# The first projection's contraction in two halves with partial sums in SBUF, and 32 instead of 16 modulation loads beside the next layer's grouped products

## The chip, the cores and the metric

The kernel runs on one core of one Trainium2 chip. The time is the device time of one execution in microseconds (us). TensorE is PE in the profile, VectorE DVE, ScalarE ACT, GpSimd POOL; SyncE (SP) only issues transfers.

## The reference

The reference computes a two-layer encoder trunk on x of 256 x 2048 (256 positions, width 2048) with a conditioning vector c of 2048. What matters here:

```python
cond = jax.nn.silu(c)
for layer in range(2):
    mod = cond @ ada_w[layer] + ada_b[layer]            # 2048 x 12288
    sh1, sc1, g1, sh2, sc2, g2 = jnp.split(mod, 6)
    h = rms_norm(x, norm_g[layer, 0]) * (1 + sc1) + sh1
    y = local_dilated_mixer(h, ...) if layer == 0 else diff_attention(h, ...)
    x = x + g1 * rms_norm(y, norm_g[layer, 1])
    h = rms_norm(x, norm_g[layer, 2]) * (1 + sc2) + sh2
    y = conv_ffn(h, ...)        # (gelu(conv(h @ gate)) * (h @ up)) @ w_down, inner width 5504
    x = x + g2 * rms_norm(y, norm_g[layer, 3])
# local_dilated_mixer: proj = h @ w_in (2048 x 3584), split into
#   qa 512, ka 256, va 256 (4 heads with a sink), qb 3 x 512, kb 512, vb 512
#   (4 heads, each over three dilations, merged); then o @ w_out (1024 x 2048)
```

Everything is in float32. Each of the weights is read once, about 580 MB in all.

## The kernel before

**Loads.** A `Plan` object fixes one sequence of 1104 loads of 512 KB each, and SP issues them in that order into a ring of nine buffers called `raw`. 720 of them are weight *units* (128 x 1024 numbers: four k-tiles by 256 columns, or two k-tiles by 512). A k-tile is 128 rows of the contraction, so the width 2048 has 16. The other 384 are rows of the modulation matrix `ada_w`, called a0, a1, ... below; the units are w0, w1, .... `put(nw, na, p)` appends nw units and na modulation loads, mixed with a slope p. A transfer starts when the load nine places earlier has been worked off and its buffer is free. The order of the sequence is also the order in which ACT and DVE work off the loads.

**A weight unit** is split into a high and a low part: ACT writes `whi` (L259), DVE writes `wlo` = `raw` - `whi` (L309), with four buffers of each. PE then makes three products, high by high, high by low and low by high, which is 24 matmuls of 256 columns (L655, L657, L658, `feat_units`: outputs with features on the partitions) or 12 of 512 (L622, L623, L624, `tok_units`: outputs with positions on the partitions).

**A modulation load** is multiplied by one column of silu(c) and added to an accumulator `aacc` (128 x 1024, two buffers) by one DVE instruction (L284; the first of a chunk is L280, or L305 on top of a tile made by POOL in L299). Sixteen such loads make one *chunk*. Then PE sums over the partitions (L459; L451 for gates), DVE adds bias and norm weights (L471, L474), and the `mod` columns of that chunk are there. ACT or DVE then makes `hf` = z * A + B (`Affine`, L509 on ACT, L511 on DVE), ACT `hT` high (L514), DVE `hT` low (L518), and only then can PE multiply by these k-tiles. A chunk of layer 0's first modulation (shift and scale, a0 to a63) serves four k-tiles. a64 to a95 are the gate, a96 to a159 the shift and scale ahead of the ConvFFN, again four k-tiles a chunk.

**Layer 0's first projection** has 56 units. Before, `GK` = (0, 4, 8, 12, 16): four groups of four k-tiles. In each group the six products va, v1 (two units), kb, qb0 and qb1 are advanced by one unit each, 6 units in all, and stay in six banks of PSUM. Each group waits until the loads up to `plan.mark[q]` are worked off and its chunk of modulation is done. After the fourth group the eight remaining outputs (4 units each) run over the whole contraction, with the attention heads between them, and ACT copies each finished output to SBUF (`feat_out`, L669). The output projection (16 units) ends the mixer, at unit w71.

**The ConvFFN of layer 0** starts with `PRE` = 7 products, grouped in the same manner: `FK` = (0, 8, 12, 16), 14, 7 and 7 units, w72 to w99. Of the 64 modulation loads that they need, 14 are gated into the norm between the two (`TAIL0`; eight loads, a132 to a139, are multiplied on PE by L272 rather than on DVE) and `PA` = 16 come among the products, by `PP` = [(12, 8), (7, 8)].

**Order.** Outside the blocks with a manual schedule a scheduler sets, at build time, the fixed order in which each engine takes its instructions, by rules of its own. So an instruction that waits holds up all that stands behind it on its engine.

At the start the norm weights `norm_g` for the gate are spread over 128 partitions by four matmuls (L1171) with four ACT copies into the tile `gb` (L1172).

Of the kernel before, what the change touches and what calls it, by code (L numbers as in the profile page):

```python
# [17 lines left out]
KT = D // P  # L18
# [8 lines left out]
OUT0 = [4, 5, 6, 7, 0, 1, 2, 3]  # L27
# [12 lines left out]
class Plan:  # L40


    def __init__(self, ab_w_in, ab_w_out, c_w_in, c_w_out, ffn_w_up, ffn_w_down):
        self.units = []
        self.held, self.native = set(), set()
# [10 lines left out]
        self.native = set(i for i in range(self.n_attn0 - 16) if NATIVE(i))  # L56
# [58 lines left out]
    def order(self):  # L115
# [4 lines left out]
        ns = [b - a for a, b in zip(GK, GK[1:])]  # L120
# [68 lines left out]
def encoder_kernel(ctx: ExitStack, tc: tile.TileContext, x, c, ada_w, ada_b, norm_g,  # L189
# [21 lines left out]
    class Stream:  # L211
        def __init__(self):
            self.loaded = self.used = self.cur = 0
            self.outstanding = self.direct = self.gate = 0
# [29 lines left out]
        def split(self, s, i):  # L244
            ap, a, n = units[i]
            v = self.raw.pop(s)
            if i in plan.native:
                self.direct += 1
                self.hl[i] = (v.rearrange("p (a n) -> p a n", a=a), None)
                return  # L250
# [61 lines left out]
        def advance(self, limit=None, lows=True, n=None):  # L312
# [43 lines left out]
        def free(self, i):  # L356
            if i in plan.native:
                self.direct -= 1
            elif i not in plan.held:
                self.outstanding -= 1  # L360
# [60 lines left out]
    grow = tmp.tile([P, 512], F32, name="junk", bufs=1)  # L421
    nc.sync.dma_start(grow[:4], norm_g[0, 1, :].rearrange("(k n) -> k n", k=4))
# [203 lines left out]
    def tok_units(dsts, act, ks, first=True, last=True, one_bank=False):  # L626

        n = 0
        while n < len(ks):
            i, (hi, lo) = st.take()  # L630
            a = hi.shape[1]
            for b in range(a):
                for t in range(2):
                    mm_tok(dsts[t], act, ks[n + b], t, hi[:, b], lo and lo[:, b],
# [4 lines left out]
    def feat_units(acc, k0, kn, n):  # L639
# [3 lines left out]
        while kt < k0 + kn:  # L643
            i, (hi, lo) = st.take()
            a = hi.shape[1]
            for b in range(a):
                k = kt + b
                for j in range(n // P):
                    wh = hi[:, b, j * P:(j + 1) * P]
                    if lo is None:  # L650
                        nc.tensor.matmul(acc[:, j], wh, cur["h"][:, k], start=k == 0 and j == 0, stop=k == KT - 1,
                                         skip_group_check=True)
                        continue
                    wl = lo[:, b, j * P:(j + 1) * P]
                    nc.tensor.matmul(acc[:, j], wh, hT[:, k, 0], start=k == 0 and j == 0, stop=False,  # L655
                                     skip_group_check=True)
                    nc.tensor.matmul(acc[:, j], wh, hT[:, k, 1], start=False, stop=False, skip_group_check=True)  # L657
                    nc.tensor.matmul(acc[:, j], wl, hT[:, k, 0], start=False, stop=k == KT - 1,  # L658
# [356 lines left out]
    def out_proj(oT, ks, l, head=None):  # L1015
# [12 lines left out]
        out_chunks(oT, ks, evac, *((2, 3) if l == 0 else (1, 2)),  # L1028
# [117 lines left out]
    with tc.tile_pool(name="at0", bufs=1, reuse_waits="tile") as pool:  # L1146
# [19 lines left out]
        sel = tmp.tile([P, 4, P], F32, name="hf", bufs=3)  # L1166
        nc.vector.tensor_copy(sel[:4], ident[:4, :4].unsqueeze(2).to_broadcast([4, 4, P]))
        mods[0, 2] = cp.tile([P, D], F32, name="gb")
        for k in range(4):
            b = bank()  # L1170
            nc.tensor.matmul(b, sel[:4, k], grow[:4], start=True, stop=True)  # L1171
            nc.scalar.activation(mods[0, 2][:, k * 512:(k + 1) * 512], b, AF.Copy)  # L1172
# [14 lines left out]
        va, kb0, qb0, qb1 = [packed() for _ in range(4)]  # L1187
        v1 = [bank(), bank()]
        for q, (k0, k1) in enumerate(zip(GK, GK[1:])):
            st.advance(plan.mark[q])  # L1190
            st.flush()
            n = k1 - k0
            for k in range(k0, k1, 4):
                for t in range(2):
                    Affine(t, k, zT[:, k:k + 4, t * P:(t + 1) * P], mods[0, 1], mods[0, 0], AFF0[t],
                           keep=bool(plan.native)).high().low()
            hT = cur["hT"]
            ks = list(range(k0, k1))
            end = k1 == KT
# [120 lines left out]
```

## Time and profile before

| what | value |
|---|---|
| median of three runs | 2292.65 us (2286.78, 2292.65, 2294.36) |
| the profiled execution | 2296.29 us, its span 2294.5 us |
| mean granted clock of PE | 0.985 |
| PE busy | 2214.2 us, 97% of the span |
| DVE busy | 1626.6 us, 71% |
| ACT busy | 1059.6 us, 46% |
| read from HBM | 582.58 MB, 255 GB/s over the span |

How to read it: PE is busy nearly all of the time, so a change can only win where PE idles or runs at a lower clock, and the slices of the span show that both happen at the front. Shares over the whole span say little about that front; it is read from windows.

### The profile page before, as it was taken

Reading aid. Unit: us, or ns where it says so; the run is one execution under the profiler, and the core shown is the slowest. Engines: PE = TensorE matmul, PEld = TensorE weight load, DVE = VectorE, ACT = ScalarE, POOL = GpSimd, SP = SyncE. Lnnn points to the kernel's source line nnn. Section 1 sums busy time; section 2 is a strip of 40 time slices with the busy share of each in tenths; the row PEclk is TensorE's granted clock in tenths of the full one; section 3 lists DMA queues with packets and bytes.
Section 4 is the critical chain, followed back from the end, with each engine's and each line's share of the span. In section 5 each row is a group of like instructions: output and inputs, shape, how many; then the busy total and the mean of one; then the engine's idle time right before and its main releaser. Section 6 shows DMA issues by size and latency. Waiting matters only on the chain.

```text
span 2294.5 us, 37387 instructions
## 1 busy us (share of the span) xinstructions
PE 2214.2 (97%) x14961; PEld 2030.4 (88%) x14961; DVE 1626.6 (71%) x1802; ACT 1059.6 (46%) x1451; POOL 45.3 (2%) x72
## 2 busy tenths in 40 slices
PE   5689999999999999999999999999999999999998
PEld 3679987999988999988789999779999888999986
DVE  7888987887766777876778986656656545565554
ACT  4344456544434444444644555455444444444443
POOL 0000000000000000000000110000000000000000
PEclk9889999999999999999999999999999999999999
DMA  9999998988889888987599986656666666666552
GB/s 342 359 326 325 327 315 284 313 295 286 286 291 303 287 287 289 297 290 235 173 347 324 302 300 201 219 169 184 203 195 204 197 205 209 193 203 203 177 188 102
DMA packets 390427, 587.14 MB, mean 256 GB/s; under 512 B 18110, under 2 KB 256360, under 8 KB 389612
## 3 DMA queue, kind: packets, MB, share of 16 engines
q1 hardware_dynamic: 390252, 584.75, 77.4%
q8 instruction: 117, 1.92, 0.3%
q14 instruction: 58, 0.48, 0.1%
HBM read 582.58 MB, written 2.10 MB: 255 GB/s over the span
## 4 chain that ended last, share of the span: by engine, by line
PE 80%; issue 12%; DVE 4%; DMA 3%; ACT 1%; POOL 1%; DVEq 0%; POOLq 0%; ACTq 0%
PE bank L655 16%; PE bank L657 16%; PE bank L658 16%; PE bank L622 9%; PE bank L624 9%; PE bank L623 9%; DVE aacc L284 2%; DMA raw<-in_ada_w_dram 2%; PE bank L459 1%; DVE wlo L309 1%; DMA raw<-in_ab_w_in_dram 1%; PE bank L523 1%; PE bank L831 1%; PE bank L794 0%; ACT junk L491 0%
## 5 line engine op out<-in xcount | busy, mean ns | idle before, releaser
L309 DVE TENSOR_TENSOR wlo<-raw,whi 128x1024 fp32r<-128x1024 f32 x708 | 861.2, 1219 | 488.6 <-ACT whi L259 472.6
L259 ACT ACTIVATE whi<-raw 128x1024 fp32r<-128x1024 f32 x708 | 745.6, 1055 | 998.7 <-PE bank L657 488.3
L655 PE MATMUL bank<-hT,whi 128*128 128x256 f32 x3616 | 1027.6, 284 | 0.0
L658 PE MATMUL bank<-hT,wlo 128*128 128x256 f32 x3616 | 1018.8, 282 | 5.4 <-DVE wlo L309 5.4
L657 PE MATMUL bank<-hT,whi 128*128 128x256 f32 x3616 | 1018.4, 282 | 0.1
L658 PEld LDWEIGHTS bank<-hT,wlo 128*128 128x128 f32 x3616 | 685.2, 189 | 7.1 <-DVE wlo L309 7.0
L655 PEld LDWEIGHTS bank<-hT,whi 128*128 128x128 f32 x3616 | 685.6, 190 | 3.1 <-ACT whi L259 1.2
L657 PEld LDWEIGHTS bank<-hT,whi 128*128 128x128 f32 x3616 | 685.4, 190 | 3.2 <-issue 1.7
L284 DVE SCALAR_TENSOR_TENSOR aacc<-raw,ccol,aacc 128x1024 f32<-128x1024 f32 x352 | 453.8, 1289 | 49.3 <-DMA raw<-in_ada_w_dram 47.5
L622 PE MATMUL bank<-whi,act 128*128 128x512 f32 x656 | 259.2, 395 | 0.0
L624 PE MATMUL bank<-whi,act 128*128 128x512 f32 x656 | 258.9, 395 | 0.0
L623 PE MATMUL bank<-wlo,act 128*128 128x512 f32 x656 | 258.9, 395 | 0.0
L624 PEld LDWEIGHTS bank<-whi,act 128*128 128x128 f32 x656 | 123.5, 188 | 29.2
L622 PEld LDWEIGHTS bank<-whi,act 128*128 128x128 f32 x656 | 123.5, 188 | 28.8
L623 PEld LDWEIGHTS bank<-wlo,act 128*128 128x128 f32 x656 | 123.5, 188 | 28.5
L622 PE MATMUL bank<-whi,hT 128*128 128x512 f32 (+1 forms) x192 | 76.1, 401 | 14.6 <-ACT hT L514 14.6
L623 PE MATMUL bank<-wlo,hT 128*128 128x512 f32 (+1 forms) x192 | 75.2, 394 | 0.0
L624 PE MATMUL bank<-whi,hT 128*128 128x512 f32 (+1 forms) x192 | 73.3, 391 | 0.0
L622 PE MATMUL bank<-whi,oT 128*128 128x512 f32 x176 | 71.1, 404 | 0.0
L623 PE MATMUL bank<-wlo,oT 128*128 128x512 f32 x176 | 69.6, 395 | 0.0
L624 PE MATMUL bank<-whi,oT 128*128 128x512 f32 x176 | 69.4, 395 | 0.0
L486 POOL TENSOR_TENSOR rs_r<-rs_m,mhalf 128x1 f32<-128x1 f32 x32 | 25.6, 809 | 1902.6 <-DVE rs_m L484 1902.6
(168 smaller groups left out, 1383.4 us busy)
## 6 DMA issues: line engine op xcount, KB each, us to landing
raw<-in_ada_w_dram SPq DMA_DIRECT2D x384, 512.0 KB, 5.6
raw<-in_ffn_w_up_dram SPq DMA_DIRECT2D x344, 512.0 KB, 4.7
raw<-in_ffn_w_down_dram SPq DMA_DIRECT2D x168, 512.0 KB, 4.9
raw<-in_c_w_in_dram SPq DMA_DIRECT2D x96, 512.0 KB, 5.3
raw<-in_ab_w_in_dram SPq DMA_DIRECT2D x56, 512.0 KB, 6.1
raw<-in_c_w_out_dram SPq DMA_DIRECT2D x32, 512.0 KB, 4.7
raw<-in_ab_w_out_dram SPq DMA_DIRECT2D x16, 512.0 KB, 5.8
gb<-in_norm_g_dram SPq DMA_DIRECT2D x3, 1024.0 KB, 4.8
```

Source lines behind the costliest of these rows:

```text
L259: nc.scalar.activation(hi, v, AF.Copy)
L284: nc.vector.scalar_tensor_tensor(self.acc, t, col, self.acc, op0=ALU.mult, op1=ALU.add)
L309: nc.vector.tensor_tensor(lo, v, hi.bitcast(F32), op=ALU.subtract)
L459: nc.tensor.matmul(t[:, j:j + 1], acc[:, j * P:(j + 1) * P], ones[:, 0:1], start=True, stop=rows is None)
L486: nc.gpsimd.tensor_tensor(r, m, mhalf, op=ALU.pow)
L523: nc.tensor.transpose(ps[:, q * P:(q + 1) * P], src[:, q * P:(q + 1) * P], ident)
L622: nc.tensor.matmul(dst, ah, hi, start=first, stop=False, skip_group_check=True)
L623: nc.tensor.matmul(dst, ah, lo, start=False, stop=False, skip_group_check=True)
L624: nc.tensor.matmul(dst, al, hi, start=False, stop=last, skip_group_check=True)
L655: nc.tensor.matmul(acc[:, j], wh, hT[:, k, 0], start=k == 0 and j == 0, stop=False, skip_group_check=True)
L657: nc.tensor.matmul(acc[:, j], wh, hT[:, k, 1], start=False, stop=False, skip_group_check=True)
L658: nc.tensor.matmul(acc[:, j], wl, hT[:, k, 0], start=False, stop=k == KT - 1, skip_group_check=True)
```

## The change

The projection is cut into k-tiles 0 to 7 and 8 to 15. In each half two groups of four k-tiles run, now with 7 units each (qb2 joins, so seven banks are held). After the first half ACT copies the seven partial sums to SBUF (`first_half`); then the seven outputs that before ran later run over k-tiles 0 to 7 (14 units), each copied to SBUF by ACT. In the second half each finished sum in PSUM is added to its partial sum by one DVE instruction (`second_half`), 14 in all, in place of the ACT copies. The partial sums of kb and qb0 to qb2 of the first head pair lie in the buffer `gb`; so the norm weights of the gate are loaded there later, by one transfer of 1 MB in `ada_finish`, and the matmuls and copies at the start go. Those of v lie in `vy`, where z was.

The b heads of the second pair move behind the a heads, and the output projection's k-tiles are reordered to match (`OUT0`, `late`). Code that had no effect (`NATIVE`, `DIRECT`, `keep`) goes.

Ahead of the ConvFFN, `PA` = 32 modulation loads are left for its products, which run in four groups of 7 units (`FK`); the eight loads multiplied on PE are now a116 to a123, and one of two `Affine` calls per group moves from DVE to ACT (`AFF1`).

```diff
-OUT0 = [4, 5, 6, 7, 0, 1, 2, 3]
+OUT0 = [4, 5, 0, 1, 2, 3, 6, 7]
...
-        for k0, k1 in zip(GK, GK[1:]):
-            self.rows(w_in0, k0, k1 - k0, 768, 256)
-            self.rows(w_in0, k0, k1 - k0, 3072, 512)
-            for c0 in (2560, 1024, 1536):
-                self.rows(w_in0, k0, k1 - k0, c0, 256)
-        for c0 in (2048, 2816, 1280, 1792, 2304, 512, 0, 256):
-            self.rows(w_in0, 0, KT, c0, 256)
-        self.token_chunks(w_out0, OUT0, late=2, lc=3)
+        for half in range(2):
+            for k0 in (8 * half, 8 * half + 4):
+                self.rows(w_in0, k0, 4, 768, 256)
+                self.rows(w_in0, k0, 4, 3072, 512)
+                for c0 in (2560, 1024, 1536, 2048):
+                    self.rows(w_in0, k0, 4, c0, 256)
+            for c0 in (512, 0, 256, 2816, 1280, 1792, 2304):
+                self.rows(w_in0, 8 * half, 8, c0, 256)
+        self.token_chunks(w_out0, OUT0, late=1, lc=3)
...
-        self.put(0, 4 * ns[0] - 3)
-        for q, n in enumerate(ns):
+        self.put(0, 13)
+        for nw in (5, 19, 5, 5):
             self.put(2, 0)
             self.put(0, 3)
             self.mark.append(len(self.seq))
-            if q < len(ns) - 1:
-                self.put(3 * n // 2 - 2, 4 * ns[q + 1] - 3, *TUNE1)
-        self.put(3 * ns[-1] // 2 - 2, 4)
+            if len(self.mark) < 4:
+                self.put(nw, 13, *TUNE1)
+        self.put(5, 4)
...
-PE_B, PE_N = 20, 8
-PP = [(12, 8), (7, 8)]
-PA = 16
+PE_B, PE_N = 36, 8
+PP = [(5, 0), (7, 16), (7, 16)]
+PA = 32
-FK = (0, 8, 12, 16)
-GK = (0, 4, 8, 12, 16)
-AFF0, AFF1 = (1, 1), (0, 1)
+FK = (0, 4, 8, 12, 16)
+AFF0, AFF1 = (1, 1), (1, 1)
...
-    grow = tmp.tile([P, 512], F32, name="junk", bufs=1)
-    nc.sync.dma_start(grow[:4], norm_g[0, 1, :].rearrange("(k n) -> k n", k=4))
...
-            if ms[0] == 5 and l == 1 and c0 == 0:
+            if (l, ms[0]) in ((0, 2), (1, 5)) and c0 == 0:
                 gate_rows(l, ms[0])
...
+    def first_half(dst, acc, scale=1.0):
+        nc.scalar.activation(dst, acc, AF.Copy, scale=scale)
+
+    def second_half(dst, part, acc, scale=1.0):
+        nc.vector.scalar_tensor_tensor(dst, acc, scale, part, op0=ALU.mult, op1=ALU.add)
...
+        early_groups(0)
+        for d, scale in late:
+            acc = packed()
+            feat_units(acc, 0, 8, 256, 0, 8)
+            first_half(d, acc, scale)
+        early_groups(1)
+
+        def rest(n):
+            d, scale = late[n]
+            acc = packed()
+            feat_units(acc, 8, 8, 256, 8, KT)
+            second_half(d, d, acc, scale)
...
+        pair(0, [kq0[:, g] for g in range(4)])
+        rest(0)
+        for j, qa in enumerate((qa0, qa1)):
+            rest(1 + j)
             for i in range(2):
                 attn_a(pool, i, 2 * j + i, qa[:, i], ka[:, j], v, j * P, oT, dists[0], sinkb)
+        for g in range(4):
+            rest(3 + g)
+        pair(1, kq1)
         out_proj(oT, OUT0, 0)
```

`early_groups(half)` is the loop over the two groups of a half: it waits for `plan.mark`, makes the `Affine` of both position halves, advances the seven products, and at the end calls `first_half` or `second_half` on the seven banks. The numbers of units before the four marks are 0, 6, 12 and 18 in the order of work before; they become 0, 7, 28 and 35.

The fixed order of instructions moves at three places. In these rows the line of the code stands first (the lines of the changed kernel differ by 10 to 20: L248 is `whi`, L273 and L269 `aacc`, L298 `wlo`, L453 and L456 the `mod` columns, L473 the squares of x for the norm, L491 `Affine`, L500 `hT` low, L511 normalised rows, L656 `second_half`), and x4 means four in a row.

ACT at the very start, before:

```order
L435 ACT_TABLE_LOAD
L435 ACTIVATE crow<-crow 16x128
L430 ACTIVATE dd<-dd 128x512
L1172 ACTIVATE gb<-bank 128x512 x4
L491 ACTIVATE junk,ssq<-xs 128x512 x6
L529 ACTIVATE hf<-xs,rs_r 128x512
```

and in the changed kernel:

```order
L417 ACT_TABLE_LOAD
L417 ACTIVATE crow<-crow 16x128
L473 ACTIVATE junk,ssq<-xs 128x512 x4
L412 ACTIVATE dd<-dd 128x512
L473 ACTIVATE junk,ssq<-xs 128x512 x4
L511 ACTIVATE hf<-xs,rs_r 128x512 x3
```

The four copies to `gb`, which stood ahead of the squares of x, are gone.

DVE around the chunk of modulation for the third group, before:

```order
L309 TENSOR_TENSOR wlo<-raw,whi 128x1024 x3
L284 SCALAR_TENSOR_TENSOR aacc<-raw,ccol,aacc 128x1024 x3
L471 TENSOR_TENSOR mod_338<-bank,abc 128x4
L280 TENSOR_SCALAR aacc<-raw,ccol 128x1024
L471 TENSOR_TENSOR mod_340<-bank,abc 128x4
L474 SCALAR_TENSOR_TENSOR mod_340<-mod_340,ngc 128x4
L284 SCALAR_TENSOR_TENSOR aacc<-raw,ccol,aacc 128x1024 x2
L518 TENSOR_TENSOR hT<-hf,hT 128x4x128
```

and now:

```order
L298 TENSOR_TENSOR wlo<-raw,whi 128x1024
L273 SCALAR_TENSOR_TENSOR aacc<-raw,ccol,aacc 128x1024
L453 TENSOR_TENSOR mod_330<-bank,abc 128x4
L273 SCALAR_TENSOR_TENSOR aacc<-raw,ccol,aacc 128x1024
L453 TENSOR_TENSOR mod_332<-bank,abc 128x4
L273 SCALAR_TENSOR_TENSOR aacc<-raw,ccol,aacc 128x1024
L456 SCALAR_TENSOR_TENSOR mod_332<-mod_332,ngc 128x4
L273 SCALAR_TENSOR_TENSOR aacc<-raw,ccol,aacc 128x1024 x2
L500 TENSOR_TENSOR hT<-hf,hT 128x4x128
```

Two accumulations of the next chunk, each with two inputs from SBUF, now stand between the three small instructions that finish the columns; before it was one with a single such input.

DVE in the products ahead of the ConvFFN, up to the last chunk's columns, before:

```order
L309 TENSOR_TENSOR wlo<-raw,whi 128x1024
L284 SCALAR_TENSOR_TENSOR aacc<-raw,ccol,aacc 128x1024 x2
L309 TENSOR_TENSOR wlo<-raw,whi 128x1024
L284 SCALAR_TENSOR_TENSOR aacc<-raw,ccol,aacc 128x1024
L309 TENSOR_TENSOR wlo<-raw,whi 128x1024
L284 SCALAR_TENSOR_TENSOR aacc<-raw,ccol,aacc 128x1024
L309 TENSOR_TENSOR wlo<-raw,whi 128x1024
L284 SCALAR_TENSOR_TENSOR aacc<-raw,ccol,aacc 128x1024
L471 TENSOR_TENSOR mod_2643<-bank,abc 128x4
L471 TENSOR_TENSOR mod_2645<-bank,abc 128x4
L474 SCALAR_TENSOR_TENSOR mod_2645<-mod_2645,ngc 128x4
L309 TENSOR_TENSOR wlo<-raw,whi 128x1024
```

and now:

```order
L298 TENSOR_TENSOR wlo<-raw,whi 128x1024
L273 SCALAR_TENSOR_TENSOR aacc<-raw,ccol,aacc 128x1024 x2
L298 TENSOR_TENSOR wlo<-raw,whi 128x1024
L273 SCALAR_TENSOR_TENSOR aacc<-raw,ccol,aacc 128x1024 x3
L298 TENSOR_TENSOR wlo<-raw,whi 128x1024
L273 SCALAR_TENSOR_TENSOR aacc<-raw,ccol,aacc 128x1024 x2
L453 TENSOR_TENSOR mod_2964<-bank,abc 128x4
L453 TENSOR_TENSOR mod_2966<-bank,abc 128x4
L456 SCALAR_TENSOR_TENSOR mod_2966<-mod_2966,ngc 128x4
L298 TENSOR_TENSOR wlo<-raw,whi 128x1024 x3
```

Where one accumulation stood beside each `wlo`, two or three stand now. From the 250th load on, the two load sequences are the same.

More of the change, by code (lines that the diff above doesn't have):

```diff
@@ L213, in __init__ @@
             self.loaded = self.used = self.cur = 0
-            self.outstanding = self.direct = self.gate = 0
+            self.outstanding = self.gate = 0
             self.ring_order = deque()
@@ L356, in free @@
         def free(self, i):
-            if i in plan.native:
-                self.direct -= 1
-            elif i not in plan.held:
+            if i not in plan.held:
                 self.outstanding -= 1
@@ L637, in tok_units, with feat_units @@
             st.done(i)
-    def feat_units(acc, k0, kn, n):
+    def feat_units(acc, k0, kn, n, begin=0, end=KT):
         hT = cur["hT"]
@@ L649, in feat_units @@
                     wh = hi[:, b, j * P:(j + 1) * P]
[L650 to L653, printed above, removed]
                     wl = lo[:, b, j * P:(j + 1) * P]
-                    nc.tensor.matmul(acc[:, j], wh, hT[:, k, 0], start=k == 0 and j == 0, stop=False,
+                    nc.tensor.matmul(acc[:, j], wh, hT[:, k, 0], start=k == begin and j == 0, stop=False,
                                      skip_group_check=True)
                     nc.tensor.matmul(acc[:, j], wh, hT[:, k, 1], start=False, stop=False, skip_group_check=True)
-                    nc.tensor.matmul(acc[:, j], wl, hT[:, k, 0], start=False, stop=k == KT - 1,
+                    nc.tensor.matmul(acc[:, j], wl, hT[:, k, 0], start=False, stop=k == end - 1,
                                      skip_group_check=True)
@@ L1165, in encoder_kernel @@
             to_columns(*row)
[L1166 to L1172, printed above, removed]
         new_hT()
@@ L1186, in encoder_kernel @@
                 chunk_T(t, ch, rs[t], zT[:, ch * 4:ch * 4 + 4, t * P:(t + 1) * P])
[L1187 to L1193, printed above, removed]
-                for t in range(2):
[L1195 to L1199, printed above, removed]
-            tok_units([va[:, 0], va[:, 1]], hT, ks, q == 0, end, one_bank=True)
-            tok_units(v1, hT, ks, q == 0, end)
-            if end:
-                v = pool.tile([P, 2, 768], F32, name="v") if plan.native else vy()
-                oT = pool.tile([P, 8, 2, S], F32R, name="oT")
-                nc.scalar.activation(v[:, :, 0:256], va, AF.Copy)
-                for t in range(2):
-                    nc.scalar.activation(v[:, t, 256:768], v1[t], AF.Copy)
-            feat_units(kb0, k0, n, 256)
-            if end:
-                kb = feat_out(pool, kb0, 1.0, "kb")
-                qb = []
-            for g, b in enumerate((qb0, qb1)):
-                feat_units(b, k0, n, 256)
-                if end:
-                    qb.append(feat_out(pool, b, QK_SCALE, f"qb{g}"))
@@ new lines, in encoder_kernel @@
+        hT = cur["hT"]
+        v = cur["h"].rearrange("p k n -> p (k n)")[:, :2 * 768].rearrange("p (t n) -> p t n", t=2)
+        kq0 = cp.tile([P, D], F32, name="gb").rearrange("p (g j n) -> p g j n", g=4, j=2)
+        kq1 = [pool.tile([P, 2, S], F32, name=n) for n in ("kb", "qb0", "qb1", "qb2")]
+        ka, qa0, qa1 = [pool.tile([P, 2, S], F32, name=n) for n in ("ka", "qa0", "qa1")]
+        late = [(ka, 1.0), (qa0, QK_SCALE), (qa1, QK_SCALE)]
+        late += [(d, QK_SCALE if g else 1.0) for g, d in enumerate(kq1)]
@@ new lines, in early_groups @@
+        def early_groups(half):
+            b0, e0 = 8 * half, 8 * half + 8
+            va, v1, kq = packed(), [bank(), bank()], [packed() for _ in range(4)]
+            for k0 in (b0, b0 + 4):
+                st.advance(plan.mark[k0 // 4])
+                st.flush()
+                for t in range(2):
+                    Affine(t, k0, zT[:, k0:k0 + 4, t * P:(t + 1) * P], mods[0, 1], mods[0, 0], AFF0[t]).high().low()
+                ks = list(range(k0, k0 + 4))
+                tok_units([va[:, 0], va[:, 1]], hT, ks, k0 == b0, k0 + 4 == e0, one_bank=True)
+                tok_units(v1, hT, ks, k0 == b0, k0 + 4 == e0)
+                for acc in kq:
+                    feat_units(acc, k0, 4, 256, b0, e0)
+            out = [(v[:, :, 0:256], va, 1.0)] + [(v[:, t, 256:768], v1[t], 1.0) for t in range(2)]
+            out += [(kq0[:, g], acc, QK_SCALE if g else 1.0) for g, acc in enumerate(kq)]
+            for d, acc, scale in out:
+                if half:
+                    second_half(d, d, acc, scale)
+                else:
+                    first_half(d, acc, scale)
@@ L1216, in encoder_kernel @@
+        early_groups(0)
+        for d, scale in late:
+            acc = packed()
+            feat_units(acc, 0, 8, 256, 0, 8)
+            first_half(d, acc, scale)
+        early_groups(1)
[3 more added lines that the diff above has]
+            feat_units(acc, 8, 8, 256, 8, KT)
+            second_half(d, d, acc, scale)
         for l in range(2):
```

38 lines of the change are left out of this document (8 added, 30 removed).

## The prediction

> **What bounds the kernel now.** I read the page first: the span and the slices.
>
> ```profile
> span 2294.5 us, 37387 instructions
> PE   5689999999999999999999999999999999999998
> DVE  7888987887766777876778986656656545565554
> DMA  9999998988889888987599986656666666666552
> ```
>
> PE is full from the fourth slice on, and before that it is not: a slice is 57 us, so the loss lies ahead of 172 us. There the transfers are full (9 in the first six slices). The front is therefore read by windows. Columns after the window's length: PE, PEld, DVE, ACT and POOL busy (instructions), the granted clock of PE, the share of the transfer engines, GB/s.
>
> ```profile
> 0.00:48.20 48.20, 20.74 (x60) 12.41 (x60) 33.16 (x48) 23.60 (x48) 4.90 (x22) 1.00 0.97 353
> 48.20:81.40 33.20, 25.61 (x138) 23.67 (x139) 29.02 (x29) 11.66 (x20) 0.00 (x0) 0.85 1.00 351
> 81.40:113.90 32.50, 21.34 (x137) 19.38 (x136) 28.35 (x27) 9.47 (x14) 1.90 (x1) 0.86 1.01 351
> 113.90:147.70 33.80, 23.36 (x136) 21.19 (x136) 29.86 (x27) 11.47 (x17) 1.90 (x1) 0.80 0.98 342
> 147.70:345.20 197.50, 197.34 (x1349) 182.39 (x1350) 174.27 (x209) 94.63 (x160) 0.59 (x2) 0.99 0.93 318
> 345.20:376.00 30.80, 30.14 (x122) 17.26 (x122) 20.59 (x31) 22.61 (x45) 4.65 (x7) 0.86 0.83 272
> 376.00:457.00 81.00, 79.86 (x669) 79.50 (x667) 66.77 (x81) 39.48 (x51) 1.90 (x1) 0.99 0.94 311
> 376.00:418.00 42.00, 42.00 (x350) 42.00 (x349) 37.30 (x42) 18.61 (x22) 0.00 (x0) 0.98 0.98 320
> 147.70:153.00 5.30, 5.13 (x18) 4.31 (x19) 4.90 (x5) 2.85 (x6) 0.00 (x0) 0.55 0.93 303
> ```
>
> The windows are cut at the starts of the four groups, at the end of unit w71 (345.2), and at unit w73 and the end of w99 (376, 457). From group to group it is 33.20, 32.50 and 33.80 us for 22 transfers each (6 units, 16 modulation loads): 99.5 / 66 = 1.51 us a transfer at a share of 0.98 to 1.01. PE has six units in that time. A unit is 24 matmuls of 256 columns, and 350 of them took 42.00 us: 2.88 us a unit, 17.3 a group. So transfers bound this front, and half of PE's time there is lost. From 147.7 to 345.2 PE bounds (197.34 of 197.50) with DVE at 88%. The seams between the groups show in PE's rows, in brackets the idle time and what ended it:
>
> ```profile
> 41.53 3.54 PE L459 MATMUL bank<-ones,aacc 128*128 128x1 f32 x16 [6.74 <-DVE aacc L284]
> 48.24 0.58 PE L622 MATMUL bank<-whi,hT 128*128 128x256 f32 x1 [3.17 <-ACT hT L514]
> 113.89 0.58 PE L622 MATMUL bank<-whi,hT 128*128 128x256 f32 x1 [5.44 <-ACT hT L514]
> 147.87 0.58 PE L622 MATMUL bank<-whi,hT 128*128 128x256 f32 x1 [5.97 <-ACT hT L514]
> ```
>
> A group starts when its chunk of modulation has gone through PE's sum, DVE's columns and ACT's `hT`.
>
> **The start: -4.5 us.** ACT at the start, then DVE's wait for it:
>
> ```profile
> 13.54 0.60 ACT L1172 ACTIVATE gb<-bank 128x512 f32<-128x512 f32 x1 [10.38 <-PE bank L1171]
> 18.66 0.60 ACT L1172 ACTIVATE gb<-bank 128x512 f32<-128x512 f32 x1 [1.11 <-PE bank L1171]
> 19.15 0.62 ACT L491 ACTIVATE junk<-xs 128x512 f32<-128x512 f32 x1
> 35.32 1.23 DVE L309 TENSOR_TENSOR wlo<-raw,whi 128x1024 fp32r<-128x1024 f32 x1 [4.56 <-ACT whi L259]
> 38.79 2.60 DVE L284 SCALAR_TENSOR_TENSOR aacc<-raw,ccol,aacc 128x1024 f32<-128x1024 f32 x2
> ```
>
> The squares start 19.15 - 13.54 = 5.6 us sooner without the copies. What follows on ACT is a chain up to the first `whi`, for which DVE idles 4.56 us, and DVE has the last accumulation of the first chunk (until 41.4) behind it. At most 5.6, at least 0 if the first transfers decide; I take the 4.5 that DVE waits. The first group starts at 48.2 - 4.5 = 43.7. The 1 MB broadcast that replaces the copies is two transfers' worth, some 3 us of SP's queue, at a place where the share is 0.93; I cost it at nothing, 3 us if that slack is gone.
>
> **The projection: -19 us in all.** Group two needs 7 + 16 = 23 transfers: 43.7 + 23 x 1.51 = 78.4. Now 21 units lie ahead of the third group, 60.5 us of PE, while 21 + 16 = 37 transfers need 55.9; so PE bounds, by little. The first unit after the seam may run at the low clock (18 matmuls in 5.13 us at 0.55, +2.4). With a seam of 3.5 (between the 3.17 and 5.97 above) the third group starts at 78.4 + 60.5 + 2.4 + 3.5 = 144.8. The fourth needs 23 transfers, 34.7 us; of these up to nine can already lie in the ring, so between 174 (DVE: 16 accumulations, 7 `wlo`, a seam) and 179.5; I take 177. At that point 35 units are done, where 18 were done at 147.7. What then remained took 197.5; it is 17 units less: 177 + 197.5 - 17 x 2.88 = 325.5.
>
> DVE's work in that stretch, by group:
>
> ```profile
> L284 DVE SCALAR_TENSOR_TENSOR aacc<-raw,ccol,aacc 128x1024 f32<-128x1024 f32 x62 | 79.3, 1279 | 0.1
> L309 DVE TENSOR_TENSOR wlo<-raw,whi 128x1024 fp32r<-128x1024 f32 x51 | 62.3, 1221 | 18.7 <-ACT whi L259 16.6 <-DMA raw<-in_ada_w_dram 2.0
> L716 DVE SCALAR_TENSOR_TENSOR smb<-dist,bank 128x512 f32<-128x512 f32 x4 | 2.7, 680 | 0.1
> ```
>
> No row shows `second_half`; L716 has the same operation and size with one input from PSUM: 14 x 0.68 = 9.5 us. ACT loses the copies of 0.6, which cost nothing. DVE has 174.3 before; now 16 accumulations fewer (-20.5), 17 `wlo` fewer (-20.8), 14 halves more: 142.5 of 148.5, 96% where it was 88%. That is the thin place: I add 1 us for waits there and for the second head pair, which now ends one unit ahead of its use in the output projection (between 0 and 3). Unit w71 ends at 326.5 instead of 345.2: -18.7, rounded -19.
>
> A seam has one more price. DVE beside POOL at the third and fourth chunk, and the same DVE operations without it:
>
> ```profile
> 108.53 1.90 POOL L299 TENSOR_TENSOR aacc<-ident,abc 128x1024 f32<-128x1024 f32 x1 [79.96 <-PE bank L459]
> 108.56 2.41 DVE L280 TENSOR_SCALAR aacc<-raw,ccol 128x1024 f32<-128x1024 f32 x1
> 141.98 1.90 POOL L299 TENSOR_TENSOR aacc<-ident,abc 128x1024 f32<-128x1024 f32 x1 [31.55 <-PE bank L459]
> 142.01 2.94 DVE L305 SCALAR_TENSOR_TENSOR aacc<-raw,ccol,aacc 128x1024 f32<-128x1024 f32 x1
> 76.57 0.74 DVE L280 TENSOR_SCALAR aacc<-raw,ccol 128x1024 f32<-128x1024 f32 x1
> ```
>
> The instruction that starts beside POOL's ends about 1.7 us late (2.41 against 0.74, 2.94 against 1.28). POOL begins when the sum over the partitions frees the accumulator, that is, just as DVE makes the columns; with two accumulations now between the columns, the seam of the third group is hit again, and the 3.5 holds it. If it were not hit, that group would come 1.7 sooner. The Trainium skill, "SBUF — State Buffer", section "Who interferes with whom", says that a DVE instruction with two SBUF inputs contends with a GpSimd one that reads SBUF, and that whoever issues first holds the shared ports while the other blocks. By that rule the accumulation between the columns would wait out POOL's 1.90 us; the two rows agree, and the rule speaks against the new order at this seam.
>
> **The products ahead of the ConvFFN: +12 us.** Nothing is saved here: the work is the same, but 16 accumulations more come after w71. Before, DVE is done with the last chunk here:
>
> ```profile
> 417.04 1.28 DVE L284 SCALAR_TENSOR_TENSOR aacc<-raw,ccol,aacc 128x1024 f32<-128x1024 f32 x1
> 425.53 0.23 DVE L471 TENSOR_TENSOR mod<-bank,abc 128x4 f32<-128x4 f32 x2 [7.21 <-PE bank L459]
> ```
>
> 418.3 is 73.1 us after w71. DVE was busy 37.30 of 42.00 from 376 on, so 4.7 us were idle; 16 x 1.28 = 20.5 more work makes it 73.1 + 20.5 - 4.7 = 88.9. Then DVE, not PE, sets the pace. Before, DVE waited 7.21 us for PE's sum, because PE had to finish its units first; PE will be waiting for DVE now, and I give back 4.1 of it. The end of w99 comes 20.5 - 4.7 - 4.1 = 11.7 later against w71 than before. Upper end 20.5, if nothing is given back. Lower end 1.5: the idle 30.80 - 20.59 = 10.2 us of DVE in the norm (345.2 to 376) would be filled too. I take 12, since the sequence puts all 32 of these loads behind the gated ones, which wait for the norm.
>
> The `Affine` moved to ACT costs nothing on PE (ACT 39.48 of 81.00 busy). Behind w99 both kernels do the same work with PE full.
>
> **Sum.** -19 + 12 = -7 us, the start being part of the 19: the span goes from 2294.5 to 2287.5. The profiled execution took 2296.29, 3.6 above the median of the three runs, 2292.65. The median goes to 2285.6, say 2285.5. About 0.3%, 6.9 us, is what a measurement can tell here from no change.
>
> **Rivals.**
> - *The later stage gives nearly everything back.* DVE runs at 96% through the rest of the projection and is late at its end, and all 20.5 us of accumulation lengthen the stage after. For it speaks DVE's 142.5 of 148.5; against it that DVE may also wait out PE. -19 + 20.5 = +1.5: 2294.
> - *The later stage costs next to nothing.* DVE fills its idle time in the norm: -19 + 1.5 = -17.5: 2275. Against it speaks the gate ahead of these loads.
> - *Slower: `second_half` holds up the attention.* Scores need q and k, and these now come from DVE, behind accumulations that wait for their transfers in a fixed order, where ACT had half its time free. If PE idles one accumulation (1.28 us) at each of the 14, it is 17.9: -7 + 17.9 = +10.9, 2303.5. It decides from 1.0 us per half on. Against it: there is a unit or more of other work between most outputs and their use.
> - *No effect.* The transfers bound everything up to the 250th load, whatever the order. 250 x 1.51 = 378 us, but the 160th accumulation ended only at 418, so 40 us of slack speak against it. 2291.
>
> **How the numbers follow.** My forecast has a chance of 0.52, and it lies at the bound of what counts: 0.30 faster, 0.22 the same; its own range is 2280 to 2291. Given back: 0.17 (0.14 the same, 0.03 slower). Costs nothing: 0.15, faster. Slower: 0.13 (0.11 slower, 0.02 the same). No effect: 0.03, the same. Faster 0.45, same 0.41, slower 0.14. The range runs from the cheap rival with the early fourth group (174 instead of 177: 2272) to just short of the slower rival, 2298.
>
> **What the changed profile would show.** First L600 at 43.7; second group at 78; PE full from there to about 141; third at 145; fourth at 177; w71 done at 326; the last accumulation of the front near 415, w99 done at 450. PE idle before L656's readers (the scores) would show the slower rival; DVE idle for transfers ahead of 415, the last one. I am wrong if the third group comes later than 150, or if the stage from w71 to w99 differs from 123.5 us by more than 8.

## The result and the profile after

| | median | runs | profiled execution | its span |
|---|---|---|---|---|
| before | 2291.63 us | 11 | 2296.29 us | 2294.5 us |
| changed | 2298.52 us | 11 | 2303.49 us | 2301.7 us |

The ratio is 1.0029, 95% interval 1.0020 to 1.0038: slower by 6.9 us, where 7 us faster was forecast, and just outside the range (2272 to 2298). The profiled execution of the changed kernel is the slowest of its eleven; the two profiles differ by 7.2 us and the medians by 6.9.

The page of the changed kernel, its span and slices as before:

```profile
span 2301.7 us, 37389 instructions
PE   4889998899999999999999999999999999999998
DVE  7779987887866777876778986557655545565555
DMA  9998989998889888987599996655666666666562
```

PE's fourth to sixth slice are full and its seventh and eighth are not: the loss has moved from the front to the stage at 327 to 464 us. The windows, cut at the starts of the four groups, the end of w71, the end of the last accumulation a159 and the end of w99 (columns as in the prediction):

```profile
0.00:44.40 44.40, 11.20 (x52) 9.47 (x52) 32.62 (x47) 21.49 (x44) 4.64 (x22) 0.83 0.99 361
44.40:78.00 33.60, 27.65 (x160) 25.98 (x161) 29.40 (x29) 12.26 (x20) 0.00 (x0) 0.77 1.06 374
78.00:144.60 66.60, 62.24 (x498) 60.23 (x497) 50.26 (x45) 32.55 (x45) 1.90 (x1) 1.00 0.95 317
144.60:176.70 32.10, 27.68 (x160) 25.73 (x160) 27.32 (x26) 12.51 (x20) 1.90 (x1) 0.79 0.98 340
176.70:327.60 150.90, 148.77 (x925) 131.31 (x926) 142.19 (x187) 70.55 (x129) 0.59 (x2) 0.99 0.89 308
327.60:426.60 99.00, 85.98 (x540) 70.40 (x540) 75.45 (x80) 45.80 (x79) 3.68 (x7) 0.91 0.91 303
426.60:464.40 37.80, 35.02 (x266) 34.76 (x266) 28.35 (x34) 22.71 (x34) 1.90 (x1) 0.88 0.97 320
```

w71 ends at 327.6 instead of 345.2, 17.6 us sooner. w99 ends at 464.3 instead of 456.9, 7.4 later. So the projection won what it was to win, and the stage ahead of the ConvFFN's main part took 136.7 us where it had taken 111.7: 25 more, not 12. That is 13 us from the 123.5 forecast, beyond the 8 that the prediction named as its sign of being wrong. Up to a159 DVE was busy 75.45 us, and idle 23.55 of 99.00; before, in the stretch from w71 to a159, it was this:

```profile
345.20:418.30 73.10, 72.44 (x472) 59.56 (x472) 58.20 (x72) 41.22 (x67) 4.65 (x7) 0.93 0.92 300
```

Busy +17.2, idle 14.9 to 23.55. DVE's idle time should have shrunk and grew. Where, DVE's waits of the changed kernel from w71 to 470 us show (in all, times, longest):

```profile
DVE wlo L298 <- ACT whi L248: 10.8, 13, 2.0
DVE mod L453 <- PE bank L441: 8.3, 2, 4.7
DVE mod L453 <- PE bank L444: 7.5, 1, 7.5
DVE aacc L273 <- DMA raw<-in_ada_w_dram: 2.8, 2, 2.5
```

The longest of them in the timelines of DVE, ACT and PE:

```profile
346.07 2.56 DVE L298 TENSOR_TENSOR wlo<-raw,whi 128x1024 fp32r<-128x1024 f32 x2 [0.58 <-ACT whi L248]
356.13 0.23 DVE L453 TENSOR_TENSOR mod<-bank,abc 128x4 f32<-128x4 f32 x2 [7.50 <-PE bank L444]
356.95 0.75 DVE L269 TENSOR_SCALAR aacc<-raw,ccol 128x1024 f32<-128x1024 f32 x1
357.06 0.49 ACT L491 ACTIVATE hf<-vy,mod,mod 128x128 f32<-128x128 f32 x1 [6.30 <-DVE mod L456]
358.13 1.22 PE L629 MATMUL bank<-hT,whi 128*128 128x256 f32 x4 [2.04 <-ACT hT L496]
```

With 32 loads left, the chunk for the second group (k-tiles 4 to 7) ends inside the norm. `PP` = [(5, 0), ...] puts five units into the sequence behind it before a128, the first of the 32. In DVE's order four `wlo` and then the columns of that chunk stand ahead of a128. DVE stands still for 7.5 us until PE has summed, with the 32 accumulations behind it; a128 itself, at 356.95, waits for no transfer (DVE even takes it ahead of the fifth unit's `wlo`, so it does not keep quite to the order of the sequence). ACT stands too (6.30), with the second position half of the first group's `hT` behind the second group's `Affine`. So PE's first product comes at 358.13, 30.5 us after w71. Before, PE's rows were these:

```profile
364.54 0.37 PE L655 MATMUL bank<-hT,whi 128*128 128x256 f32 x1
371.79 0.58 PE L655 MATMUL bank<-hT,whi 128*128 128x256 f32 x1
```

The first is 19.3 us after w71, but only six matmuls ran there before PE went on with its sums. The products ran on from 371.79, 26.6 us after w71, so PE's start is some 4 us later now, not 11.

### The profile page after: what moved, and what is told of

Read it like the earlier page. It is cut to its first block, busy times and chain, and to the rows that moved or that the text cites. A ratio compares the mean times of both kernels' runs of the same rounds, so it can differ in the third digit from the quotient of the medians.

```text
span 2301.7 us, 37389 instructions
## 1 busy us (share of the span) xinstructions
PE 2213.9 (96%) x14953; PEld 2031.8 (88%) x14953; DVE 1630.3 (71%) x1799; ACT 1064.8 (46%) x1463; POOL 44.1 (2%) x72
## 4 chain that ended last, share of the span: by engine, by line
PE 81%; issue 9%; DVE 5%; DMA 3%; ACT 2%; POOL 0%; DVEq 0%; POOLq 0%; SPq 0%; ACTq 0%
PE bank L631 16%; PE bank L632 16%; PE bank L629 16%; PE bank L600 10%; PE bank L601 10%; PE bank L602 10%; DMA raw<-in_ada_w_dram 2%; DVE aacc L273 2%; DVE wlo L298 1%; PE bank L441 1%; ACT hf L491 1%; PE bank L775 1%; ACT junk L473 1%; PE bank L812 0%; ACT whi L248 0%
## 5 line engine op out<-in xcount | busy, mean ns | idle before, releaser
L248 ACT ACTIVATE whi<-raw 128x1024 fp32r<-128x1024 f32 x708 | 745.4, 1055 | 998.1 <-PE bank L631 486.6
L298 DVE TENSOR_TENSOR wlo<-raw,whi 128x1024 fp32r<-128x1024 f32 x708 | 861.2, 1220 | 483.7 <-ACT whi L248 469.2
L632 PE MATMUL bank<-hT,wlo 128*128 128x256 f32 x3616 | 1021.6, 283 | 10.5 <-DVE wlo L298 10.5
L273 DVE SCALAR_TENSOR_TENSOR aacc<-raw,ccol,aacc 128x1024 f32<-128x1024 f32 x352 | 455.5, 1294 | 55.3 <-DMA raw<-in_ada_w_dram 53.6
L601 PEld LDWEIGHTS bank<-wlo,act 128*128 128x128 f32 x656 | 123.5, 188 | 28.9
```

Of the source, the lines that this page charges most:

```text
L248: nc.scalar.activation(hi, v, AF.Copy)
L273: nc.vector.scalar_tensor_tensor(self.acc, t, col, self.acc, op0=ALU.mult, op1=ALU.add)
L298: nc.vector.tensor_tensor(lo, v, hi.bitcast(F32), op=ALU.subtract)
L601: nc.tensor.matmul(dst, ah, lo, start=False, stop=False, skip_group_check=True)
```

## The experiments

All were timed in five rounds beside the kernel before. "w71" and "w99" are the ends of those units in each kernel's profile, "a159" the end of the last accumulation; "-" where records of the trace are missing. Each ratio is to the runs of before in the same rounds (medians of 2290.66 to 2291.83 us); a difference of two medians given below would come out up to some 2 us otherwise by the ratios.

| kernel | median us | ratio to before (95%) | w71 | a159 | w99 |
|---|---|---|---|---|---|
| before | 2291.63 | | 345.2 | 418.3 | 456.9 |
| changed | 2298.52 | 1.0029 (1.0020, 1.0038) | 327.6 | 426.6 | 464.3 |
| e1 projection only | 2294.57 | 1.0012 (1.0002, 1.0021) | 348.1 | 419.7 | 457.8 |
| e2 front only | 2317.86 | 1.0109 (1.0095, 1.0123) | 348.3 | 443.0 | - |
| e3 start only | 2289.23 | 0.9989 (0.9978, 0.9999) | 343.2 | 414.9 | 453.4 |
| e4 24 left | 2299.88 | 1.0032 (1.0020, 1.0043) | 336.8 | 426.1 | 462.7 |
| e5 changed, 16 short | 2293.11 | 1.0011 (1.0001, 1.0022) | 321.7 | 416.4 | 453.9 |
| e6 before, 16 short | 2290.46 | 0.9997 (0.9988, 1.0006) | 343.9 | 414.1 | 452.8 |
| e7 no add on DVE | 2292.75 | 1.0007 (0.9998, 1.0016) | 323.1 | 418.9 | 456.3 |
| e8 start, 12 left | 2297.20 | 1.0032 (1.0019, 1.0044) | 346.8 | 416.3 | 460.5 |
| e9 changed, no PE rows | 2293.75 | 1.0016 (1.0007, 1.0025) | 326.7 | 420.4 | 456.0 |
| e10 changed, three groups | 2288.92 | 0.9988 (0.9977, 0.9998) | 325.9 | 415.1 | 451.2 |
| e11 start, Affine on ACT | 2290.42 | 0.9997 (0.9988, 1.0006) | 341.0 | 415.7 | 454.8 |
| e12 start, no PE rows | 2297.07 | 1.0025 (1.0015, 1.0036) | 343.1 | 418.1 | 461.4 |
| e13 before, four groups | 2291.73 | 1.0003 (0.9994, 1.0012) | 343.1 | 419.2 | 457.4 |
| e14 front, three groups | 2310.12 | 1.0085 (1.0071, 1.0099) | 348.7 | 439.9 | - |
| e15 three groups, 24 left | 2297.21 | 1.0031 (1.0020, 1.0042) | 332.6 | 425.5 | 461.3 |
| e16 three groups, no PE rows | 2291.90 | 1.0008 (0.9999, 1.0017) | 328.5 | 418.1 | 455.5 |

One reading runs through the table: w99 ends 35.6 to 39.1 us after a159 in 14 of the 16 kernels where both are known (e8 and e12, at 44.2 and 43.3, are the exceptions). In that time PE is nearly full (35.02 of 37.80 us in the changed kernel) and works off the units that are still left. That DVE's last accumulation dates the stage does not follow from it. Where 32 loads are left, e5 and e7 below speak for DVE's work. In the kernel before PE is full, as the prediction's row of 42.00 of 42.00 us shows, and e6 below finds nothing to gain on DVE.

**The two parts alone (e1, e2).** e1 is the changed kernel with

```diff
-PE_B, PE_N = 36, 8
-PP = [(5, 0), (7, 16), (7, 16)]
-PA = 32
-FK = (0, 4, 8, 12, 16)
-AFF0, AFF1 = (1, 1), (1, 1)
+PE_B, PE_N = 20, 8
+PP = [(12, 8), (7, 8)]
+PA = 16
+FK = (0, 8, 12, 16)
+AFF0, AFF1 = (1, 1), (0, 1)
```

and e2 the kernel before with the reverse.

> The changed kernel with the old split ahead of the ConvFFN (16 modulation loads left, groups of 14, 7 and 7 units, one Affine on DVE), so the projection's change alone. Theory A (the gain of the projection is real, but DVE has no room for 16 more accumulations there): DVE is busy 142.2 of 150.9 us between the fourth group and w71; 20.5 us more do not fit, w71 ends 12 to 16 us later than in the changed kernel, at 340 to 343, and the stage behind takes its old 111.7: 2 to 5 us faster than before, 2287 to 2290. Theory B (the two edits add up): w71 stays at 327.6, w99 ends 17.6 sooner than before, 2274.

> The kernel before with only the new split ahead of the ConvFFN (32 loads left, four groups of 7). Theory A and B: w71 stays near 345, since PE bounds the projection, and the stage to w99 takes 25 us more, 2316. Rival C (the stage cost more than forecast because the changed kernel reaches it 17.6 us early, ahead of its transfers): here it takes only some 12 more, 2303, with no wait of DVE for transfers.

e1: 2294.57, slower than either theory said. e1 runs with the changed kernel up to the fourth group and then loses all of it; from there to w71:

```profile
175.60:348.10 172.50, 157.04 (x941) 138.88 (x941) 160.56 (x206) 69.89 (x128) 0.59 (x2) 0.94 0.92 318
```

172.5 us, where the changed kernel took 150.9: +21.6 for 16 accumulations of 20.5 (DVE busy 18.4 more). DVE's 8.7 us of idle time there took up none of them; 12 us stay idle with the 16 added. PE loses with it: it waits 5.4 us for a transfer of the convolution's bias (0.5 in the changed kernel) and 2.5 for ACT, and its granted clock is 0.94, not 0.99. So in this order a DVE that was 94% busy had no room left, and theory B falls; how much of the 21.6 is DVE's work and how much what its lateness does to transfers and clock is not parted. In e1 the projection's gain of PE time and the place of the 16 loads could not be had together. e2: 2317.86, +26 as expected from A and B; from w71 to a159 it took 94.7 us (348.3 to 443.0) where before took 73.1 and the changed kernel 99.0. So it is not the early arrival that makes the stage dear (rival C).

**The start alone (e3).** The kernel before without the matmuls and copies of the norm weights:

```diff
-            if ms[0] == 5 and l == 1 and c0 == 0:
+            if (l, ms[0]) in ((0, 2), (1, 5)) and c0 == 0:
...
-        for k in range(4):
-            b = bank()
-            nc.tensor.matmul(b, sel[:4, k], grow[:4], start=True, stop=True)
-            nc.scalar.activation(mods[0, 2][:, k * 512:(k + 1) * 512], b, AF.Copy)
```

> The kernel before with only the start changed: norm weights of the gate by one late transfer of 1 MB instead of matmuls and ACT copies. If the 4 us at the start carry through the groups that transfers bound: every group 4 us sooner, w71 and w99 too, 2287 to 2288. If a later wait swallows them: 2291 to 2292.

2289.23, 2.6 us faster than the 2291.83 of before beside it; in the profile the first group starts at 44.69 instead of 48.24, w71 ends 2.0 us sooner, a159 3.4 and w99 3.5. The term holds, at 3.5 rather than 4.5.

**Less DVE work (e5, e6, e7).** In e5 (changed) and e6 (before):

```diff
+            elif 68 <= i < 80 or 84 <= i < 88:
+                nc.vector.scalar_tensor_tensor(self.acc[:, :64], t[:, :64], col, self.acc[:, :64], op0=ALU.mult, op1=ALU.add)
```

and in e7 (changed):

```diff
     def second_half(dst, part, acc, scale=1.0):
-        nc.vector.scalar_tensor_tensor(dst, acc, scale, part, op0=ALU.mult, op1=ALU.add)
+        nc.scalar.activation(dst, acc, AF.Copy, scale=scale)
```

> The changed kernel with 16 accumulations right behind the fourth group (a68 to a79, a84 to a87) cut to 64 of their 1024 columns; the rest of these products is left out. All transfers, units and sums stay. It takes some 16 x 1.1 = 17 us from DVE. Theory D (from the fourth group to w99 DVE's total work sets the end, whichever stage it stands in): w99 comes 12 to 17 us sooner, 2282 to 2287. Rival T (transfers set it): no change, 2298. Rival S (the seams set it, with DVE waiting at them): at most 4 us, 2295.

> The kernel before with the same 16 accumulations cut to 64 of 1024 columns, the rest left out. Theory D says that DVE still had room there (174.3 of 197.5 busy, PE full): 0 to 4 us, 2288 to 2292. If DVE bounds it as well: 12 to 17 us sooner, 2275 to 2280.

> The changed kernel with the 14 sums of the second half copied to SBUF by ACT; the addition of the first half's partial sum is left out. It takes 14 x 0.68 = 9.5 us from DVE and puts 14 copies of 0.6 on ACT. Theory D: 7 to 10 us sooner, 2289 to 2291, PE's wait for q and k gone too. Rival (the halves are hidden): no change, 2298.

e5 gained 5.4 us and e7 5.8 on the changed kernel (2298.52), in the profiles 10.5 and 8.0 at w99; e6 gained 1.1 on before, inside the noise. The profile of the changed kernel is its slowest execution, 5.0 us above its median, and that of e5 its fastest, 6.0 below, so the two profiles differ by more than the medians (their spans by 16.3 us). So DVE's work counts in the changed kernel and not measurably in the kernel before, but theory D is too simple: e5 took 16 us away (278 instead of 1278 ns each) and moved w71 by 5.9 only. With less on DVE, PE becomes the bound of that stage, as the window of e7 from the fourth group to w71 shows:

```profile
175.30:323.10 147.80, 147.27 (x925) 131.47 (x926) 134.57 (x173) 76.95 (x143) 0.59 (x2) 0.99 0.91 315
```

PE is full for all but half a microsecond. The 14 additions of 9.5 us cost 4.5 at w71.

**How many loads to leave (e4, e8, e15).** e4 is the changed kernel with `PA = 24`, `PP = [(5, 0), (7, 8), (7, 16)]`, `PE_B = 24`; e8 is e3 with `PA = 12`, `PP = [(12, 6), (7, 6)]`, `PE_B = 18`; e15 is e10 (below) with `PA = 24`, `PP = [(12, 8), (7, 16)]`, `PE_B = 24`.

> The changed kernel with 24 instead of 32 modulation loads left, the first 8 of the PE's set now in the chunk of k-tiles 8 to 11. Theory A by work: 8 accumulations (10.2 us) move back into the projection, where 8.7 us of DVE are idle: w71 at 328 to 332; the stage behind gets 10.2 us cheaper, +15 instead of +25: w99 level with before or 3 sooner, 2289 to 2292. If the loss is the extra seams (DVE waiting 12.2 us for PE's sums) and not the work, the stage stays at +22 to +25: 2296 to 2299.

> The kernel before with the late norm weights at the start and 12 instead of 16 modulation loads left for the products ahead of the ConvFFN. Theory D: 4 accumulations (5.1 us) move to a stage where DVE has 23 us idle and PE bounds, and the stage behind w71 gets up to 5 us cheaper: 2284 to 2287. If PE's units decide the end of that stage, no change against the late norm weights alone: 2289.

> The changed kernel with three groups and 24 instead of 32 loads left. If DVE's work sets both stages, 8 accumulations (10.2 us) moved between them change nothing: 2287 to 2291. If the later stage has the larger seam, 2282 to 2286; if w71 comes 9 us later as it did with 24 loads and four groups and the stage gives only half of it back, 2292 to 2295.

e4 2299.88, e8 2297.20, e15 2297.21: none gained, and all three are slower than any of their expectations. In e4 and e15 w71 came 9.2 and 6.7 us later, against 10.2 for 8 accumulations; in e4 the stage gave all of it back (125.9 us from w71 to w99, where the changed kernel has 136.7), in e15 none of it (128.7 against 125.3). In both, PE works off seven loads, not eight: the trace has 28 matmuls of L261 instead of 32, since a128, the first of its chunk, goes to DVE. e8 lost 8 us against e3; there PE waits 4.6 us for `hT` from DVE at the first products behind the norm, where e3 has no such wait. Common to these three is that a chunk ends in the middle of the gated loads instead of with them, as with 16 and 32; that this is the reason was not tried.

**The loads on PE (e9, e12, e16).** In each `PE_N` is 0: no load is worked off on PE, in the changed kernel (e9), in e3 (e12), in e10 (e16).

> The changed kernel with the eight modulation loads a116 to a123 worked off on DVE instead of PE. On PE the 32 matmuls of L261 (13.7 us at 0.43 each) and the 16 of L444 go from the norm between w71 and w73; on DVE 8 x 1.28 = 10.2 us come, where it is idle 14.2 of 28.5 us. If the seam is the long chain on PE (L261, L441, L444 up to 355.7, and DVE's 7.5 us of waiting for it): w73 4 to 8 us sooner, w99 as much, 2291 to 2295. If DVE's work sets the pace there too: w73 level, w99 0 to 8 later, 2298 to 2306.

> The kernel before with the late norm weights at the start and no modulation load on PE (a132 to a139 on DVE). Before, PE spends 14.4 us on these loads between w71 and w73 and DVE idles 10.2 us there. If PE's chain sets the time to w73: 3 to 8 us sooner than with the late norm weights alone, 2281 to 2286. If DVE's work does: 0 to 6 later, 2289 to 2295.

> The changed kernel with three groups, and the eight loads of the norm on DVE instead of PE. With four groups that gained 4.8 us, with the old projection it lost 8. If PE's chain (L261 and L444, 12 us between the last transposes and the first products) is what the second group waits for: 2282 to 2286. If DVE's 10.2 us of further work are: 2292 to 2299.

e9 gained 4.8 us, e12 lost 7.8 against e3, e16 lost 3.0 against e10. With the loads gone, PE waits for ACT's normalised rows instead: 12.2 us in e9, 10.8 in e12 and 11.1 in e16 (0.7 in e3). So most of PE's work on these loads filled time in which it would have waited for ACT, and DVE gets 10.2 us more to do. That only e9 gained fits its DVE having stood still for PE's chain; it is argued, not shown.

**The groups ahead of the ConvFFN (e10, e11, e13, e14).** The `Affine` that the change also moves to ACT was tried alone in e11, which is e3 with `AFF1` = (1, 1). It took 2290.42, 1.2 us more than e3, where 2 to 4 less had been expected if DVE's order delayed the seams: no gain. e10 is the changed kernel, with its 32 loads, in three groups:

```diff
-PP = [(5, 0), (7, 16), (7, 16)]
+PP = [(12, 16), (7, 16)]
-FK = (0, 4, 8, 12, 16)
+FK = (0, 8, 12, 16)
```

e14 is e2 with the same two lines; e13 is the kernel before with `FK = (0, 4, 8, 12, 16)` and `PP = [(5, 0), (7, 8), (7, 8)]`.

> The changed kernel with the products ahead of the ConvFFN in three groups (14, 7 and 7 units) as before, and 32 loads left still: the 16 of k-tiles 8 to 11 among twelve units. If the waits of DVE at the two seams cost (12.2 us, of which the second is 4.7): PE has 14 units at hand while DVE works off the next chunk, and w99 comes 2 to 6 us sooner, 2292 to 2296. If the work of DVE alone sets it: no change, 2298.

> The kernel before with four groups of 7 units ahead of the ConvFFN and 16 loads left as ever. Here the chunk of the second group is finished before the norm. Theory E (a group costs only where its chunk ends in the norm, so that DVE and PE stand at its columns): 0 to 2 us slower than before, 2291 to 2293. Rival F (each further group costs its seam anywhere): 6 to 10 us slower, 2297 to 2301.

> The kernel before with 32 loads left but three groups (14, 7, 7). With four groups it took 2317.9. Theory E: the seam's 9 to 13 us come back, 2305 to 2309, still 13 to 17 slower than before, since PE bounds the old projection and gains nothing from the 16 accumulations that leave it. Rival (the seam is tied to the new projection): 2317.

e10: 2288.92, 9.6 us faster than the changed kernel, more than the 2 to 6 expected, and faster than before by 0.12% (0.02 to 0.23%). It beats both, though before only barely and no more than e3 does, so beyond what the start alone gives, the rest of the change has won nothing that can be measured. Its profile is its fastest execution (2283.79). w71 ends 1.7 us sooner than in the changed kernel, and a159 11.5. DVE at the same place:

```profile
337.41 1.28 DVE L273 SCALAR_TENSOR_TENSOR aacc<-raw,ccol,aacc 128x1024 f32<-128x1024 f32 x1 [1.60 <-DMA raw<-in_ada_w_dram]
338.67 0.75 DVE L269 TENSOR_SCALAR aacc<-raw,ccol 128x1024 f32<-128x1024 f32 x1
342.83 1.28 DVE L273 SCALAR_TENSOR_TENSOR aacc<-raw,ccol,aacc 128x1024 f32<-128x1024 f32 x1 [3.42 <-DMA raw<-in_ada_w_dram]
352.98 0.23 DVE L453 TENSOR_TENSOR mod<-bank,abc 128x4 f32<-128x4 f32 x2 [2.99 <-PE bank L444]
```

a128 (L269) starts at 338.67 instead of 356.95; three further accumulations and two `wlo` are done ahead of the columns, and these wait 2.99 instead of 7.50. The other two sets of columns in this stage, first the changed kernel, then e10:

```profile
394.53 0.23 DVE L453 TENSOR_TENSOR mod<-bank,abc 128x4 f32<-128x4 f32 x2 [4.72 <-PE bank L441]
430.11 0.23 DVE L453 TENSOR_TENSOR mod<-bank,abc 128x4 f32<-128x4 f32 x2 [3.54 <-PE bank L441]
383.22 0.23 DVE L453 TENSOR_TENSOR mod<-bank,abc 128x4 f32<-128x4 f32 x2 [3.09 <-PE bank L441]
417.18 0.23 DVE L453 TENSOR_TENSOR mod<-bank,abc 128x4 f32<-128x4 f32 x2 [2.10 <-PE bank L441]
```

Both kernels make three sets behind w71; before made two, with waits of 4.66 and 7.21. The waits of DVE in this stage, against those above:

```profile
DVE wlo L298 <- ACT whi L248: 6.9, 8, 1.7
DVE mod L453 <- PE bank L441: 5.2, 2, 3.1
DVE aacc L273 <- DMA raw<-in_ada_w_dram: 5.0, 2, 3.4
DVE mod L453 <- PE bank L444: 3.0, 1, 3.0
```

and its windows from w71 to a159 and to w99:

```profile
325.90:415.10 89.20, 83.40 (x544) 69.30 (x543) 74.48 (x79) 46.39 (x79) 3.68 (x7) 0.92 0.99 337
325.90:451.20 125.30, 117.04 (x804) 102.50 (x804) 102.82 (x114) 68.77 (x112) 5.57 (x8) 0.92 0.99 336
```

DVE's work is the same (74.48 against 75.45); its idle time up to a159 is 14.7 us instead of 23.55. At the columns it waits 8.2 instead of 15.8 us in this stage and for `whi` 6.9 instead of 10.8, for transfers 5.0 instead of 2.8. The edit of e10 does two things at once: it joins two groups, and it moves a128 ahead of the first unit in the sequence, where the changed kernel has five units without a modulation load. No run parts the two, say by four groups with loads among the first five units.

e13: 2291.73, no change, as theory E says: with 16 loads left the second group's chunk is finished before the norm, and four groups cost nothing that can be measured. e14: 2310.12, 7.7 less than e2 and 1 us more than expected, so the seam is not tied to the new projection, and the 16 accumulations still cost 19 where the old projection wins nothing by their going.

## Why the prediction was wrong

**The start and the four groups: right.** Forecast were 43.7, 78, 145, 177. PE's rows at the first and the third group, then the others:

```profile
44.50 0.58 PE L600 MATMUL bank<-whi,hT 128*128 128x256 f32 x1 [3.70 <-ACT hT L496]
144.74 0.39 PE L600 MATMUL bank<-whi,hT 128*128 128x256 f32 x1 [4.14 <-ACT hT L496]
78.06 0.29 PE L600 MATMUL bank<-whi,hT 128*128 128x256 f32 x1
176.82 0.39 PE L600 MATMUL bank<-whi,hT 128*128 128x256 f32 x1 [0.65 <-ACT hT L496]
```

The last two rows are the second and the fourth. From the first group to the second it is 33.6 us for 23 transfers, 1.46 each where 1.51 was taken. The start itself came 3.7 us sooner than before, not 4.5.

**POOL beside DVE: right.**

```profile
137.73 1.90 POOL L288 TENSOR_TENSOR aacc<-ident,abc 128x1024 f32<-128x1024 f32 x1 [119.48 <-PE bank L441]
137.76 2.94 DVE L273 SCALAR_TENSOR_TENSOR aacc<-raw,ccol,aacc 128x1024 f32<-128x1024 f32 x1
```

Again 2.94, ahead of the columns. The Trainium skill ("SBUF — State Buffer", section "Who interferes with whom") says that a DVE instruction with two SBUF inputs contends with a GpSimd one that reads SBUF. The trace agrees: 2.94 us beside POOL's 1.90, where the same instruction takes 1.28 without it.

**The end of the projection: right in size.** w71 at 327.6 against 326.5 forecast. DVE was busy 142.19 us (forecast 142.5).

**The products ahead of the ConvFFN, "+12 us": wrong, and it is the step that failed.** It counted 16 accumulations (20.5) and let them fill DVE's idle time (-4.7), for 88.9 us from w71 to a159. It took 99.0. The work came out smaller (+17.2, since the Affine that went to ACT leaves DVE too), but idle time grew by 8.7 instead of shrinking. I had priced the work of the loads that move and not the waits that come with them. The 16 loads bring a third set of columns behind w71, and with four groups and the first five units bare of modulation loads DVE had nothing in its order to do while PE summed the first: 7.50 us. DVE's order is fixed at build time, so this could be read ahead of any run: the second group's columns stand ahead of a128 there. I had looked only at the last chunk's.

With three groups, e10 measures 89.20 for the 88.9, and 13.6 more than before to w99 for the 11.7. That the sum fits e10 is luck: there the work grew by 16.3, not 20.5, and DVE's idle time (14.9 before, 14.7 in e10) was not filled at all.

After a159 it took 37.8, not 34.5. I gave back 4.1 us of the wait of 7.21 for the last columns. That wait did fall, to 3.54, but PE still had its units to do, busy 35.02 of the 37.80 us, and a159 to w99 went only from 38.6 to 37.7. Together 1.1 (w71) + 10.1 (to a159) + 3.3 (behind it) = 14.5 us, which is what lies between -7 and +7.4.

**The rivals.** The nearest was "gives nearly everything back" (+1.5). It was right that nothing of the 20.5 would be filled, but the stage cost 25, and it put the loss into DVE's 96% in the projection, where w71 was on time. That thin place is real, as e1 and e7 show. The slower rival, the halves holding up the attention, was not what made the kernel slower: the waits for L656 that PE shows come to 0.9 us in all, not 17.9. Yet the halves cost 5.8 us against copies by ACT (e7), where I had 1.

**Left open:** whether the fourth group or the five units without loads made the seam dear; why 24 and 12 loads are worse than 16 and 32; and why w71 came 3.1 us later in e2, although 16 accumulations had left its projection.

## What to carry to other kernels

Where PE, DVE and the transfers are all close to full, work that one engine saves only counts if the next one can take it up: sum the work and the waits of the engine that is nearest to its limit (here DVE) over both stages, instead of PE's units stage by stage. When a split moves or adds a step that waits for another engine, price that wait apart from the work: the waiting instruction holds all that stands behind it, so ask what stands ahead of it in the order. And idle time in small waits on other engines is not room: in e1 a DVE at 94% took up none of 16 further accumulations.

## What the runs showed of the hardware

From the first group to the second the transfers ran at 351 GB/s and a share of 1.00 in the kernel before, and at 374 GB/s and 1.06 in the changed one: a share of 1.00 in this view is not the most that the engines can do. Why the second is higher, these runs do not show.

The instructions behind w99, the same in these kernels (from 40 us behind it on ACT and DVE run the same list in the same order), took 1830.8 us in the profile of e10, 1834.1 in that of e3 and 1837.4 and 1837.6 in those of the changed kernel and of before. So executions differ by up to 7 us where nothing differs in the program, as much as the whole effect here.
